# Rounding the convolved rows to their high part on ScalarE instead of VectorE, in the recurrent block of a two-layer diffusion backbone

## The chip, the cores and the metric

The kernel runs on one core of one Trainium2 chip. The metric is the device time of one launch in microseconds (us). A trace of one profiled execution gives start, length and idle time of each instruction on the engines: TensorE (PE, with its weight loads as PEld), VectorE (DVE), ScalarE (ACT), GpSimd (POOL) and SyncE (SP), which issues the DMAs. Each engine takes its instructions in the order in which the program wrote them; a wait at the head of an engine's queue holds everything behind it.

## What is computed

Two layers over 256 latent rows with a prefix of 256 context rows, width 1024. Layer 0 is neighbourhood attention and a dense SwiGLU. Layer 1, in which the change lies, is a bidirectional gated linear recurrence (1536 channels), followed by a top-2-of-8 expert SwiGLU. Cut to the recurrent block:

```python
g, xr = jnp.split(h @ w_in, 2, axis=-1)             # 1536 + 1536 columns
xc = dwconv(xr, conv_w, conv_b)                     # width 4, per channel
for d, rev in enumerate((False, True)):             # both directions
    r = sigmoid(blockdiag(xc, wa[d], ba[d]))        # 16 blocks of 96x96
    i = sigmoid(blockdiag(xc, wx[d], bx[d]))
    log_a = -8.0 * r * softplus(-lam[d])
    a, mult = exp(log_a), sqrt(-expm1(2.0 * log_a))
    hs += linear_scan(a, mult * (i * xc), h0, rev)  # h0: the context's last state
y = (gelu(g) * hs) @ w_out
```

## The kernel before

Matrix products with full precision are made of three passes. An operand is split into a high part (rounded to float32r) and a low part (the operand minus its high part), and `mm3` (lines 468 to 472) multiplies high by high, high by low and low by high. For weights, ScalarE makes the high part `whi` (line 370) from a landed tile `raw`, and VectorE the low part `wlo` (line 381); five such pairs are alive at a time.

The recurrent block holds its 1536 channels as 12 tiles of 128 channels by 512 columns (256 latent, 256 context). `MIX` (line 48) is the order in which the block is written down, and so the order on each engine: `g` is a tile of the gelu branch, `x` a tile of the convolved branch, `a` the gates of three tiles, `w` the output product.

`g0-4 x0-2 g5 a0 x3-5 g6-8 a1 x6-8 g9-10 x9 a2 x10-11 g11 a3 w...`

`x_tile(t)` multiplies (`pX`, PE), lets ScalarE do the convolution's centre tap with the bias (line 1387, `xcv`), VectorE the three other taps (line 1389, three instructions), and splits `xcv` into `xcs`: the high part (line 1395) and the low part (line 1396). `gates(q)` takes three x tiles through 12 block-diagonal products in PSUM (`pA`, 4 banks in turn); ScalarE empties each bank with a tanh (line 1423, `ri`), makes a second tanh from every other one (line 1426, `th`, 7 buffers), and VectorE multiplies (line 1429). A bank or a `th` buffer that is still in use holds up whoever wants it next.

`post(q)` puts the rest of the three tiles into a list, `todo`, from which `run(n)` writes pieces between later tiles: `rates` (Exp on ScalarE at line 1442, then lines 1443 and 1444 on VectorE), `roots` (Sqrt on ScalarE at line 1436, then line 1437 on VectorE), `scans` (lines 1448 to 1454, VectorE alone), `gated` (line 1461, `z`). So the leftovers of one group of tiles stand between the x tiles of the next. In particular the piece after x tile 3, 6 or 10 begins with Exp on ScalarE, preceded by a load of ScalarE's function table; and the scans of a group are written before x tile 9 while the gates of the group a2 are written after it.

Of the kernel before, what the change touches and what calls it, by code (L numbers as in the profile page):

```python
# [419 lines left out]
def body(tc, nc, es, a, out, upto, dbg):  # L420
# [940 lines left out]
    def win_mm(t, p, s):  # L1361
        u = st.need(("win", t))
        for k in range(KD):
            mm3(p, wt(u, k), hx(k, s), k == 0, k == KD - 1)
        st.done(("win", t))
# [14 lines left out]
    def x_tile(t):  # L1380
        p = psu("pX")
        win_mm(12 + t, p, slice(0, 512))
        xc_ = xv.tile([P, 512], F32, name="xcv", tag="xcv", bufs=4)
        o = xc_.rearrange("p (s t) -> p s t", s=2)
        r = p.rearrange("p (s t) -> p s t", s=2)
        cw = vv("cw", 4 * t, 4)
        nc.scalar.activation(o, r, AF.Identity, bias=vv("cb", t, 1), scale=cw[:, 2:3])
        for j, (d0, d1, s0, s1) in ((0, (2, NL, 0, NL - 2)), (1, (1, NL, 0, NL - 1)), (3, (0, NL - 1, 1, NL))):
            nc.vector.scalar_tensor_tensor(
                o[:, :, d0:d1], r[:, :, s0:s1], cw[:, j:j + 1], o[:, :, d0:d1], ALU.mult, ALU.add  # L1390
            )
        if t % 2 == 0:
            xs2[0] = rawm.tile([P, 2, 2, 512], F32R, name="xcs", tag="raw", bufs=RM // 2)
        xh, xl_ = xs2[0][:, t % 2, 0], xs2[0][:, t % 2, 1]
        nc.vector.tensor_copy(xh, xc_)
        nc.vector.tensor_tensor(xl_, xc_, xh.bitcast(F32), ALU.subtract)
        xc_t[t] = (xc_, xh, xl_)

# [111 lines left out]
    for i, (kind, n) in enumerate(MIX):  # L1510
# [3 lines left out]
        elif kind == "x":  # L1514
            if n == 0:
                st.lag = 0
                lp = pool(ls, "lp", 2)
                vs = ExitStack()
                xv = pool(vs, "xv", side="right")
            x_tile(n)  # L1520
            if n == 11:
                st.add_pool(hp, 4, wide=True)
# [551 lines left out]
```

## Time and profile before

| | us |
|---|---|
| median of 3 runs (lowest, highest) | 1827.32 (1821.88, 1831.45) |
| profiled execution | 1827.48 |
| its span, first to last instruction | 1825.5 |
| PE busy | 1733.7 (95%) |
| DVE busy | 1064.1 (58%) |
| ACT busy | 752.9 (41%) |
| POOL busy | 92.1 (5%) |

The shares are means over stages with different limits. The change lies between 726 and 913 us, in the recurrent block; from about 1050 us on the expert weights are streamed at 419 GB/s. A stage is read from its own stretch of the trace: which engine has no idle time in it, and what the others wait for. A row of the timeline gives start, length, engine, line, operation and tile, how many instructions are merged in it, and in brackets the idle time of the engine before it with what ended that.

### The profile page before, as it was taken

Reading aid. Unit: us, or ns where it says so; the run is one execution under the profiler, and the core shown is the slowest. Engines: PE = TensorE matmul, PEld = TensorE weight load, DVE = VectorE, ACT = ScalarE, POOL = GpSimd, SP = SyncE. Lnnn points to the kernel's source line nnn. Section 1 sums busy time; section 2 is a strip of 40 time slices with the busy share of each in tenths; the row PEclk is TensorE's granted clock in tenths of the full one; section 3 lists DMA queues with packets and bytes.
Section 4 is the critical chain, followed back from the end, with each engine's and each line's share of the span. In section 5 each row is a group of like instructions: output and inputs, shape, how many; then the busy total and the mean of one; then the engine's idle time right before and its main releaser. Section 6 shows DMA issues by size and latency. Waiting matters only on the chain.

```text
span 1825.5 us, 26013 instructions
## 1 busy us (share of the span) xinstructions
PE 1733.7 (95%) x9973; PEld 1289.3 (71%) x9973; DVE 1064.1 (58%) x1698; ACT 752.9 (41%) x1147; POOL 92.1 (5%) x126
## 2 busy tenths in 40 slices
PE   8999899999999999989898999999899999998997
PEld 6887568988788889877687766666566556655564
DVE  4784676886766437699878444453344344534342
ACT  4434654422222226666736433333334333433341
POOL 1001341200000003000010000000000000000000
PEclk9999999999999999999898999999999999999999
DMA  7444621364656223232475799999999999999996
GB/s 305 168 142 147 204 75 47 127 209 163 229 196 231 92 93 102 96 113 76 162 274 207 298 413 419 420 419 420 419 419 419 420 420 419 420 419 419 419 420 277
DMA packets 94963, 489.87 MB, mean 268 GB/s; under 512 B 10480, under 2 KB 15984, under 8 KB 55920
## 3 DMA queue, kind: packets, MB, share of 16 engines
q1 hardware_dynamic: 94688, 488.01, 68.9%
q8 instruction: 80, 1.31, 0.3%
q14 instruction: 51, 0.42, 0.1%
q10 hardware_dynamic: 144, 0.13, 0.0%
HBM read 487.05 MB, written 1.05 MB: 267 GB/s over the span
## 4 chain that ended last, share of the span: by engine, by line
PE 61%; DMA 24%; DVE 10%; ACT 3%; issue 1%; POOL 1%; SPq 0%; DVEq 0%; ACTq 0%; POOLq 0%
DMA raw<-moe_d 23%; PE ph L1808 10%; PE psa L470 4%; PE psa L471 4%; PE psa L472 4%; PE pY L1492 2%; PE pF L470 2%; PE pF L471 2%; PE pF L472 2%; PE ph L1896 2%; PE ph L1898 2%; PE ph L1897 2%; DVE wlo L381 2%; PE py L1828 1%; PE py L1829 1%
## 5 line engine op out<-in xcount | busy, mean ns | idle before, releaser
L381 DVE TENSOR_TENSOR wlo<-raw,whi 128x1024 fp32r<-128x1024 f32 x386 | 461.7, 1221 | 217.2 <-ACT whi L370 213.7
L370 ACT CAST whi<-raw 128x1024 fp32r<-128x1024 f32 x388 | 395.7, 1047 | 251.2 <-DMA raw<-moe_d 100.2
L1808 PE MATMUL ph<-raw,xs 128*64 128x256 f32 x2240 | 267.2, 390 | 33.7 <-ACT msil L1925 33.7
L1808 PEld LDWEIGHTS ph<-raw,xs 128*64 128x64 f32 x2240 | 155.7, 139 | 126.4 <-ACT msil L1925 47.8
L470 PE MATMUL psa<-hh,whi 128*128 128x512 f32 (+1 forms) x384 | 145.1, 378 | 0.0
L471 PE MATMUL psa<-hl,whi 128*128 128x512 f32 (+1 forms) x384 | 144.2, 376 | 0.7 <-DVE hl L721 0.6
L472 PE MATMUL psa<-hh,wlo 128*128 128x512 f32 (+1 forms) x384 | 143.8, 374 | 0.0
L1898 PE MATMUL ph<-wlo,xe 128*128 128x512 f32 x336 | 132.6, 395 | 4.4 <-DVE wlo L381 4.4
L1896 PE MATMUL ph<-whi,xe 128*128 128x512 f32 x336 | 134.2, 399 | 0.9 <-ACT whi L370 0.9
L1897 PE MATMUL ph<-whi,xe 128*128 128x512 f32 x336 | 131.9, 393 | 0.0
L1808 PE MATMUL ph<-raw,mgs 128*64 128x512 f32 (+1 forms) x608 | 128.1, 563 | 0.6 <-ACT mgs L1871 0.5
L1927 DVE TENSOR_TENSOR msil<-msil,ph 128x256 f32<-128x256 f32 x35 | 14.6, 418 | 157.3 <-PE ph L1808 144.0
L595 DVE SCALAR_TENSOR_TENSOR macc<-raw,c,macc 128x1024 f32<-128x1024 f32 x84 | 105.3, 1280 | 0.7
L1808 PEld LDWEIGHTS ph<-raw,mgs 128*64 128x64 f32 x608 | 40.6, 137 | 68.0 <-issue 63.2
L470 PEld LDWEIGHTS psa<-hh,whi 128*128 128x128 f32 x384 | 73.5, 191 | 14.4 <-issue 2.1
L471 PEld LDWEIGHTS psa<-hl,whi 128*128 128x128 f32 x384 | 73.5, 191 | 13.6 <-DVE hl L721 1.5
L472 PEld LDWEIGHTS psa<-hh,wlo 128*128 128x128 f32 x384 | 73.4, 191 | 12.6
L1898 PEld LDWEIGHTS ph<-wlo,xe 128*128 128x128 f32 x336 | 63.5, 189 | 20.0 <-DVE wlo L381 6.4
L470 PE MATMUL pF<-gh,whi 128*128 128x512 f32 (+1 forms) x208 | 74.8, 360 | 0.4 <-ACT gh L483 0.4
L471 PE MATMUL pF<-gl,whi 128*128 128x512 f32 (+1 forms) x208 | 74.3, 357 | 0.3 <-DVE gl L484 0.3
L483 ACT CAST mgh<-pgt 128x512 fp32r<-128x512 f32 x21 | 12.3, 586 | 150.5 <-PE pgt L1874 150.5
L472 PE MATMUL pF<-gh,wlo 128*128 128x512 f32 (+1 forms) x208 | 74.1, 356 | 0.0
(349 smaller groups left out, 3051.9 us busy)
## 6 DMA issues: line engine op xcount, KB each, us to landing
raw<-moe_d SPq DMA_DIRECT2D x304, 1024.0 KB, 17.4
raw<-f_d SPq DMA_DIRECT2D x66, 512.0 KB, 3.6
raw<-wm_d SPq DMA_DIRECT2D x64, 512.0 KB, 4.6
raw<-moe_d SPq DMA_DIRECT2D x60, 512.0 KB, 17.4
raw<-wmh_d SPq DMA_DIRECT2D x32, 512.0 KB, 8.1
raw<-qkv_d SPq DMA_DIRECT2D x24, 512.0 KB, 4.2
raw<-win_d SPq DMA_DIRECT2D x24, 512.0 KB, 3.5
raw<-gat_d SPq DMA_DIRECT2D x14, 512.0 KB, 3.7
```

The lines of the kernel that those rows point to most:

```text
L370: self.nc.scalar.copy(hi, self.raws[i][0])
L381: eng.tensor_tensor(lo, self.take(key), hi.bitcast(F32), ALU.subtract)
L470: nc.tensor.matmul(o, w[0], x[0], start=first, stop=False)
L471: nc.tensor.matmul(o, w[0], x[1], start=False, stop=False)
L472: nc.tensor.matmul(o, w[1], x[0], start=False, stop=last)
L595: nc.vector.scalar_tensor_tensor(m[2][s], w, c32[:, k, s:s + 1], m[2][s], ALU.mult, ALU.add)
L1492: nc.tensor.matmul(Y[m][:, 0:NL], u[:, (t % 8) * P:(t % 8) * P + P], z_t[k], start=(k == 0), stop=(k == NB - 1))
L1808: nc.tensor.matmul(o[h], x, w[h], start=first, stop=last, skip_group_check=True)
L1828: nc.tensor.matmul(ys[e][n], x[0], w[0], start=b, stop=False)
L1896: nc.tensor.matmul(acc[part], xh[:, k], w[0], start=(k == 0), stop=False)
L1897: nc.tensor.matmul(acc[part], xl_[:, k], w[0], start=False, stop=False)
L1898: nc.tensor.matmul(acc[part], xh[:, k], w[1], start=False, stop=(k == 7))
```

## The change

One line of `x_tile` is changed: the copy that rounds `xcv` to its high part is issued on ScalarE and no longer on VectorE.

```diff
         xh, xl_ = xs2[0][:, t % 2, 0], xs2[0][:, t % 2, 1]
-        nc.vector.tensor_copy(xh, xc_)
+        nc.scalar.copy(xh, xc_)
         nc.vector.tensor_tensor(xl_, xc_, xh.bitcast(F32), ALU.subtract)
```

It takes 12 instructions from VectorE's queue and puts 12 into ScalarE's, each at the place where it was written: behind line 1387 of its own tile, and ahead of whatever ScalarE does next. It reads `xcv` after VectorE's last tap, and VectorE's subtraction reads what it writes. The queues of PE, POOL and SP are the same.

ScalarE at x tile 3, the first tile after the gates a0 (`whi` is a weight's high part, `ri` the gate to be exponentiated):

```order
 L370 CAST whi<-raw 128x1024
 L1387 ACTIVATE xcv<-pX,vec 128x512
+L1395 CAST xcs<-xcv 128x512
 L1442 ACT_TABLE_LOAD
 L1442 ACTIVATE ri_6867<-ri_6867,sp_656 128x512
```

The table load and the Exps of `rates` now stand behind the cast; x tiles 6 and 10 read alike.

ScalarE at x tile 9, the tile ahead of the gates a2 (`pA` are the gate products in PSUM):

```order
 L370 CAST whi<-raw 128x1024
 L1387 ACTIVATE xcv<-pX,vec 128x512
+L1395 CAST xcs<-xcv 128x512
 L1423 ACTIVATE ri_7719<-pA,hb 128x512
 L1426 ACTIVATE th<-ri_7719,sp_655 128x512
```

Here the instruction that follows is the first that empties a bank of `pA` for the gates a2.

VectorE at the same x tile 9:

```order
 L1389 SCALAR_TENSOR_TENSOR xcv<-pX,vec,xcv 128x2x254
 L1389 SCALAR_TENSOR_TENSOR xcv<-pX,vec,xcv 128x2x255 x2
-L1395 CAST xcs<-xcv 128x512
 L1396 TENSOR_TENSOR xcs<-xcv,xcs 128x512
 L1429 SCALAR_TENSOR_TENSOR ri_7730<-ri_7730,xcv 128x512
```

The cast leaves, and nothing comes between the last tap and the subtraction; the same holds for all 12 tiles.

## Rows read from the trace of the kernel before

**Rows 1.** Chain that ended last, in order of time: start, length, what.

```profile
898.73 0.82 ACT th L1426
...
900.17 0.79 PE pA L470
```

**Rows 2.** Busy time by engine from x tile 3 to the last gates.

```profile
766.51:912.45 145.94, 127.95 (x596) 104.95 (x595) 135.63 (x202) 102.94 (x139) 0.00 (x0) 0.95 0.32 110
```

**Rows 3.** SP's DMA queue behind the last gates: a wait, and the issue.

```profile
SPq L305 <- PE pA L472: 3.7, 1, 3.7
...
910.95 1.84 SPq L305 DMA_DIRECT2D raw<-moe_d  x3
```

**Rows 4.** The line of the cast: count, then shortest, median, longest in ns.

```profile
L1395 DVE CAST xcs<-xcv x12: 426/428/429, 730.5 to 882.0; 128x512 fp32r<-128x512 f32 x12
```

**Rows 5.** Timeline, ACT and DVE, another split of 128x512 (layer 0's SwiGLU).

```profile
347.75 0.62 ACT L483 CAST gh<-fg 128x512 fp32r<-128x512 f32 x1 [0.83 <-DVE fg L1253]
...
348.41 0.69 DVE L484 TENSOR_TENSOR gl<-fg,gh 128x512 fp32r<-128x512 f32 x1 [0.69 <-ACT gh L483]
```

**Rows 6.** Timeline, DVE, x tile 2, then x tiles 3 to 5.

```profile
738.15 2.31 DVE L1389 SCALAR_TENSOR_TENSOR xcv<-pX,vec,xcv 128x508 f32<-128x508 f32 x3 [0.80 <-ACT xcv L1387]
...
767.33 2.31 DVE L1389 SCALAR_TENSOR_TENSOR xcv<-pX,vec,xcv 128x508 f32<-128x508 f32 x3 [3.30 <-ACT xcv L1387]
...
770.74 0.68 DVE L1443 SCALAR_TENSOR_TENSOR ri<-ri,th 128x512 f32<-128x512 f32 x1
...
776.13 2.31 DVE L1389 SCALAR_TENSOR_TENSOR xcv<-pX,vec,xcv 128x508 f32<-128x508 f32 x3
...
781.67 1.29 DVE L1437 TENSOR_TENSOR ri<-ri,th 128x512 f32<-128x512 f32 x2
...
784.01 2.31 DVE L1389 SCALAR_TENSOR_TENSOR xcv<-pX,vec,xcv 128x508 f32<-128x508 f32 x3
...
789.83 1.22 DVE L381 TENSOR_TENSOR wlo<-raw,whi 128x1024 fp32r<-128x1024 f32 x1
```

**Rows 7.** ACT's table load, Exp and Sqrt lines, and one weight cast.

```profile
767.31 1.28 ACT L1442 ACT_TABLE_LOAD   x1
...
781.87 1.03 ACT L370 CAST whi<-raw 128x1024 fp32r<-128x1024 f32 x1
...
L1442 ACT ACTIVATE ri<-ri,sp x24: 799/803/818, 768.6 to 915.1; 128x512 f32<-128x512 f32 x24
...
L1436 ACT ACTIVATE th<-th x24: 612/618/637, 775.9 to 919.9; 128x512 f32<-128x512 f32 x24
```

**Rows 8.** Timeline, ACT, gates a2 and x tile 10.

```profile
840.85 0.69 ACT L1423 ACTIVATE ri<-pA,hb 128x512 f32<-128x512 f32 x1 [0.28 <-PE pA L472]
...
851.94 0.81 ACT L1426 ACTIVATE th<-ri,sp 128x512 f32<-128x512 f32 x1 [7.00 <-DVE th L1454]
...
869.63 0.78 ACT L1387 ACTIVATE xcv<-pX,vec 128x512 f32<-128x512 f32 x1
```

**Rows 9.** Timeline, DVE, x tile 9 and x tile 10.

```profile
857.54 2.31 DVE L1389 SCALAR_TENSOR_TENSOR xcv<-pX,vec,xcv 128x508 f32<-128x508 f32 x3
...
870.86 2.31 DVE L1389 SCALAR_TENSOR_TENSOR xcv<-pX,vec,xcv 128x508 f32<-128x508 f32 x3
```

**Rows 10.** Timeline, PE, gates a2: products 5 to 7, and the eighth.

```profile
846.09 0.39 PE L470 MATMUL pA<-xcs,whi 128*128 128x512 f32 x1
...
849.95 0.39 PE L472 MATMUL pA<-xcs,wlo 128*128 128x512 f32 x1
854.32 0.79 PE L470 MATMUL pA<-xcs,whi 128*128 128x512 f32 x1 [3.99 <-ACT ri L1423]
```

**Rows 11.** Timeline, DVE and ACT, behind x tile 11.

```profile
885.20 1.29 DVE L1437 TENSOR_TENSOR ri<-ri,th 128x512 f32<-128x512 f32 x2
...
887.54 2.49 DVE L1437 TENSOR_TENSOR ri<-ri,th 128x512 f32<-128x512 f32 x4
...
882.41 0.39 ACT L1376 ACTIVATE ge<-pG 128x256 f32<-128x256 f32 x1
```

## The prediction, made blind

> **What bounds the kernel now.** I read the chain of waits first. From 767 us to 898.7 us nearly every link is a VectorE instruction; then it passes over ScalarE's tanh of line 1426, which had waited for a scan, to PE's gate products [rows 1]. The table of busy time says the same: from x tile 3 to the last gates VectorE works 135.63 of 145.94 us, ScalarE 102.94, PE 127.95 [rows 2]. So in this stretch the end is set by VectorE's queue, and PE, whose 95% over the whole span suggests otherwise, waits. Before x tile 3 VectorE still has air. After the last gates PE is the bound, and the first expert weights are issued only when PE has done with its last gate products [rows 3]. Every later load hangs on buffers that later work frees, so I count a delay of the last gates in full at the end.
>
> **What the change takes away.** 12 casts of 428 ns [rows 4]; with the hand-over to the next instruction each holds VectorE's queue for 0.46 us. That is 5.5 us, 4.1 us of it (9 tiles) on the chain.
>
> **What it adds per tile: a round trip.** The kernel has the same three steps elsewhere: in layer 0 VectorE multiplies, ScalarE casts 128x512 in 0.62 us, VectorE subtracts, and VectorE sits idle 0.69 us in between [rows 5]. Hand-overs cost 0.03 to 0.04 us each. In x_tile nothing stands between the last tap and the subtraction on VectorE, so VectorE waits 0.69 us where it worked some 0.49 us: 0.2 us worse per tile, before anything is queued up.
>
> **What it adds to ScalarE's queue.** Until now ScalarE did its centre tap and ran ahead; now it stands still until VectorE has finished that tile's three taps. What it does next comes late, and much of that is what VectorE or PE wants next. I follow that tile by tile.
>
> *x tiles 0 to 2.* The round trips, and weight casts that come behind them, cost VectorE a few tenths at each tile. The idle 0.80 us ahead of tile 2's taps [rows 6] takes up most, and the 3.30 us ahead of tile 3's taps show that VectorE is not yet the bound; I carry 0.4 us (bounds 0 to 0.8) into gates a0, whose products PE runs without a break up to x tile 3.
>
> *x tiles 3 to 5, on the chain.* Tile 3: the taps end at 767.33 + 2.31 = 769.64, and line 1443 followed at 770.74 [rows 6], because ScalarE had already loaded its table (767.31) and made Exp during the taps. Now cast (0.62), table load (1.28) and Exp (0.80) [rows 7] come one after the other behind the taps: 0.03 + 0.62 + 0.02 + 1.28 + 0.02 + 0.80 + 0.04 = 2.81 us instead of 1.10, **1.7 us late**. Tile 4: the taps end at 778.44 + 1.7 = 780.14, cast to 780.79, the fifth and sixth Exp to 782.35, table load to 783.64, first Sqrt (0.62) to 784.28; line 1437 starts at 784.32 instead of 781.67, **2.65 late**. ScalarE's second Sqrt ends at 784.81 and its weight cast (1.03, here 1.05) at 785.78; VectorE's `wlo` at 785.82 is 2.94 late. Tile 5: taps end at 786.32 + 2.94 = 789.26, cast to 789.91, four Sqrts to 792.12 (line 1437 follows each), weight cast to 793.1; VectorE's `wlo` at 793.14 instead of 789.83, **3.3 us late**. The scans behind it need nothing of ScalarE, and the `th` buffers and low weights that PE waits for come from this queue, so everything shifts by 3.3.
>
> *x tiles 6 to 8.* The same instructions in the same order: another 3.3 us. With the 0.4 from the start VectorE is 7.0 us late at tile 9.
>
> *x tile 9.* This is the largest term. ScalarE is done with the centre tap before 840.85, but VectorE comes to the other taps only at 857.54, behind the scans of the group before [rows 8, 9]. So far ScalarE uses that time: at 840.85 it begins to empty the banks of gates a2, and has emptied three when it stops at 851.94 for a `th` buffer (7.00 us of idle). PE gets through seven of the 12 products and stands 3.99 us until 854.32 [rows 10]. With the cast ahead of line 1423, ScalarE empties nothing until VectorE has reached and done the taps: 857.54 + 2.31 + 7.0 = 866.85, plus cast 0.65, plus the first emptying 0.69, with hand-overs 868.25. PE, with all four banks full, starts again there and not at 854.32: 13.9 late, and with eight products to do instead of five. Products 5 to 7 took 846.09 to 850.2 [rows 10], 4.1 us. The rest up to x tile 10's product is PE's own work then as now, so ScalarE's tap for tile 10 moves from 869.63 by 13.9 + 4.1 = **18.0 us**. VectorE, which had 0.4 us of backlog there, starts the taps of 870.86 17.6 late. The tile thus costs 10.6 beyond the 7.0.
>
> *x tiles 10 and 11.* Tile 10 repeats tile 3, 1.7. Tile 11 repeats the first half of tile 4, 0.95. Then the gelu tile g11 stands between the Sqrts: after the second Sqrt ScalarE has a weight cast (1.03), a table load (1.28), gelu (0.39), a table load (1.28) and the third Sqrt (0.62), 4.6 us [rows 7, 11]. Until now this ran beside VectorE; line 1437 came at 885.20 and again at 887.54, 2.34 apart [rows 11]. With ScalarE no longer ahead the gap is 4.6 us and some 0.5 for the second Sqrt, 5.1 us: 2.75 more. VectorE's last scans start 17.6 + 1.7 + 0.95 + 2.75 = 23.0 us late, and with them the `th` at 898.73 and PE at 900.17 [rows 1]. ScalarE comes to that tanh some 5 us before its buffer is free, so nothing else is later.
>
> **Sum.** 0.4 + 3.3 + 3.3 + 10.6 + 1.7 + 0.95 + 2.75 = 23.0 us. On the profiled execution's own 1827.48 (span 1825.5 and 2.0 around it), which is 0.2 us off the median of the runs shown, that gives 1850.5; I say 1850.
>
> **Unknown costs.** The clock: after the 4 us stop PE's first products took up to 0.79 us instead of 0.39 [rows 10], and the granted clock of the stage averages 0.95 [rows 2], so part of it ran at the lower level, 1.2 GHz. Whether a stop of some 16 us leaves PE there longer no row shows; between nothing and the length of products 5 to 7 (0 to 4 us), I take nothing beyond what the row after the shorter stop already holds, since by then ScalarE's emptyings also pace PE. At the far end the expert stage may give something back if loads run further ahead; bounds 0 to half the delay, I take 0 by [rows 3].
>
> **Rivals.** (1) *VectorE was the bound and is relieved.* 5.5 us less work, up to 4.1 of it on the chain: 1822 to 1823.5, which is not slower, and too little to be told from no change. The place is the pair last tap and subtraction; it decides if VectorE has at least 0.7 us of other work to do between them, or ScalarE's later work is never awaited. The order shows neither: the subtraction is the next instruction in all 12 tiles. The Trainium skill's Perfetto Trace Analysis, section Optimizing Scalar/DVE Operations, says that with DVE saturated, moving work to Scalar may make sense, and that DVE is faster where it has a performance mode. By that rule the time would be this rival's; the trace supports its premise (VectorE saturated) and also its caution (0.43 against 0.62 us), but the rule prices engine time and not the wait. (2) *Only the round trip counts*, ScalarE being idle enough to catch up: 12 x 0.2 = 2.4 us, 1830, no change that can be told. Against it: the Exp and the emptyings are awaited at once. (3) *Tile 9 costs only a round trip*, if gates a2 were held by the `th` buffers or VectorE anyway: 23.0 - 10.6 + 0.2 = 12.6, 1840. For it: ScalarE does stand 7.00 us there already. Against it: three banks were emptied before that stop. (4) *Half the delay is given back* in the expert stage: 1839. (5) *PE's lower clock and missed overlaps add* some 4 to 8 us: 1856. That the change does not do what it says is ruled out by the order of instructions.
>
> **How the numbers follow.** Forecast 0.62 (1845 to 1855), rival 3 0.13, rival 4 0.06, rival 5 0.08, rival 2 0.08, rival 1 0.03. The range 1837 to 1857 takes in the forecast, rivals 3 and 4 and about half of 5, and leaves out some 0.15. A measurement of this kernel tells about 0.5% (9 us) from no change, so rivals 1 and 2 are "same", 0.12 with some allowance for the measurement: faster 0.02, same 0.12, slower 0.86.
>
> **What would show it.** In the profile of the changed kernel: line 1395 on ScalarE 12 times at about 0.62 us, its waits for line 1389 long, the longest (over 15 us) at tile 9; line 1396 waiting 0.69 us for it; line 1443 waiting some 1.7 us for Exp at tiles 3, 6 and 10; PE standing 14 to 18 us for line 1423 in gates a2; the first expert load near 934 instead of 911. The forecast is wrong if PE's stop in gates a2 is under 8 us, if line 1443 finds Exp ready, or if the expert stage takes less time than before from its first load on.

## The result, and the profile after

The changed kernel takes 1849.87 us (median of 4 runs, 1848.37 to 1850.44), the kernel before in the same comparison 1827.86. The ratio is 1.0126, 95% interval 1.0109 to 1.0144: some 22 us slower, between 20 and 26. The profiled execution took 1848.37 with a span of 1846.4, 20.9 over the span before. In what follows, medians leave out the few launches that took 2466.94 us or more.

The cast of line 1395 as a group: duration, then what ended the idle time of its engine, then who waited for it.

```profile
L1395 ACT CAST xcs<-xcv x12: 617/620/622, 729.5 to 901.0; 128x512 fp32r<-128x512 f32 x12
its engine sat idle before it (us, times) until:
  DVE xcv L1389: 47.6, 12
who waited for it (us, times):
  DVE xcs L1396: 8.9, 12
...
  PE pA L470: 2.1, 1
```

The cast itself is 7.4 us of work in all. ScalarE stands 47.6 us in front of it, waiting for the taps. VectorE waits 0.74 us for each cast, against the 0.43 us that its own cast took [rows 4].

VectorE's timeline, x tiles 3 to 11 (start, length, instruction, count, idle time ahead and who ended it); its rows answer to [rows 6, 9, 11].

```profile
767.11 2.31 DVE L1389 SCALAR_TENSOR_TENSOR xcv<-pX,vec,xcv 128x508 f32<-128x508 f32 x3 [3.29 <-ACT xcv L1387]
770.17 0.69 DVE L1396 TENSOR_TENSOR xcs<-xcv,xcs 128x512 fp32r<-128x512 f32 x1 [0.74 <-ACT xcs L1395]
772.30 0.69 DVE L1443 SCALAR_TENSOR_TENSOR ri<-ri,th 128x512 f32<-128x512 f32 x1 [1.44 <-ACT ri L1442]
...
784.10 1.29 DVE L1437 TENSOR_TENSOR ri<-ri,th 128x512 f32<-128x512 f32 x2 [0.43 <-ACT th L1436]
...
863.83 2.30 DVE L1389 SCALAR_TENSOR_TENSOR xcv<-pX,vec,xcv 128x508 f32<-128x508 f32 x3
...
888.02 2.31 DVE L1389 SCALAR_TENSOR_TENSOR xcv<-pX,vec,xcv 128x508 f32<-128x508 f32 x3 [3.30 <-ACT xcv L1387]
...
910.10 2.50 DVE L1437 TENSOR_TENSOR ri<-ri,th 128x512 f32<-128x512 f32 x4 [2.41 <-ACT th L1436]
```

In the kernel before, none of the rows that answer to these but the first, 767.33, waited. Now VectorE waits for ScalarE at Exp, at Sqrt, at x tile 10's centre tap and behind the gelu tile. The taps of x tile 3 start within 0.22 us of where they did, those of x tile 10 17.2 us later.

The timeline of ScalarE around x tile 9 (centre tap, cast, first emptying) answers to [rows 8]:

```profile
850.87 0.79 ACT L1387 ACTIVATE xcv<-pX,vec 128x512 f32<-128x512 f32 x1
...
866.22 0.62 ACT L1395 CAST xcs<-xcv 128x512 fp32r<-128x512 f32 x1 [14.56 <-DVE xcv L1389]
866.75 0.68 ACT L1423 ACTIVATE ri<-pA,hb 128x512 f32<-128x512 f32 x1
```

And PE's, in gates a2, answers to [rows 10]:

```profile
848.88 0.80 PE L470 MATMUL pA<-xcs,whi 128*128 128x512 f32 x1 [3.77 <-ACT ge L1376]
...
867.48 0.80 PE L470 MATMUL pA<-xcs,whi 128*128 128x512 f32 x1 [11.79 <-ACT ri L1423]
```

Line 1423 is the first emptying of a gate's bank. It stands behind the cast, the cast behind the taps, and the taps behind the scans of the group before. Before, ScalarE had emptied three banks while VectorE was at those scans. Now it empties none, and PE stands twice: 3.77 us for a bank that a late gelu still holds, then 11.79 us until 867.48 instead of 854.32. SP's queue issues the first expert load 21.7 us later than in [rows 3]:

```profile
932.64 1.84 SPq L305 DMA_DIRECT2D raw<-moe_d  x3
```

### The profile page after: what moved, and what is told of

Same layout as the page of the kernel before. It is cut to its first block, busy times and chain, and to the rows that moved or that the text cites. A ratio compares the mean times of both kernels' runs of the same rounds, so it can differ in the third digit from the quotient of the medians.

```text
span 1846.4 us, 26007 instructions
## 1 busy us (share of the span) xinstructions
PE 1737.0 (94%) x9973; PEld 1290.7 (70%) x9973; DVE 1059.9 (57%) x1686; ACT 759.6 (41%) x1159; POOL 92.5 (5%) x126
## 4 chain that ended last, share of the span: by engine, by line
PE 59%; DMA 25%; DVE 9%; ACT 5%; issue 1%; POOL 1%; SPq 0%; DVEq 0%; ACTq 0%; POOLq 0%
DMA raw<-moe_d 24%; PE ph L1808 9%; PE psa L470 4%; PE psa L471 4%; PE psa L472 4%; PE pY L1492 2%; PE pF L470 2%; PE pF L471 2%; PE pF L472 2%; PE ph L1898 2%; PE ph L1896 2%; PE ph L1897 2%; DVE wlo L381 2%; PE psa L1168 1%; PE psa L1170 1%
## 5 line engine op out<-in xcount | busy, mean ns | idle before, releaser
L470 PE MATMUL pA<-xcs,whi 128*128 128x512 f32 x112 | 48.4, 432 | 29.9 <-ACT ri L1423 18.7
```

The costliest lines, as they stand in the source:

```text
L470: nc.tensor.matmul(o, w[0], x[0], start=first, stop=False)
```

## Which part of it costs what

Executions differ ahead of this stretch: among the profiled ones, programs that are alike up to there reach the taps of x tile 3 anywhere between 762.17 and 768.41 us. So the table counts from the start of these taps (T) in each trace, to the taps of x tiles 9 and 10, to the last four Sqrt products (the row `L1437 ... x4` above, other line numbers elsewhere) and to SP's first expert load (`moe_d`). The last column is from there to the end of the span. Each entry is the difference of two starts, the last column that of a start and the end of the span. What such a difference is worth can be read off too: with x tile 11 alone nothing is changed between T and the taps of x tile 10, and yet they come 0.12 us later than in the kernel before, and as late with x tiles 0 to 2, whose changes lie ahead of T.

| Kernel | T | to x9 | to x10 | to last Sqrt products | to first expert load | the rest |
|---|---|---|---|---|---|---|
| before | 767.33 | 90.21 | 103.53 | 120.21 | 143.62 | 914.55 |
| after (all 12) | 767.11 | 96.72 | 120.91 | 142.99 | 165.53 | 913.76 |
| x tiles 0 to 2 | 764.31 | 90.32 | 103.65 | 120.33 | 143.96 | 915.33 |
| x tiles 3, 6, 10 | 767.12 | 93.85 | 107.41 | 125.86 | 148.63 | 915.15 |
| x tiles 4, 5, 7, 8 | 766.06 | 93.24 | 106.56 | 123.23 | 145.86 | 914.08 |
| x tile 9 | 765.02 | 90.40 | 114.49 | 131.18 | 154.59 | 914.99 |
| x tile 11 | 762.17 | 90.32 | 103.65 | 123.95 | 145.09 | 913.84 |
| all but x tile 9 | 765.12 | 96.88 | 110.21 | 132.29 | 155.00 | 917.78 |
| added work, not held | 771.36 | 90.32 | 103.64 | 120.31 | 143.86 | 915.18 |
| added work, held | 764.89 | 98.76 | 122.83 | 144.73 | 167.36 | 914.05 |
| later place, ScalarE | 770.44 | 86.85 | 99.87 | 115.72 | 138.18 | 913.88 |
| later place, VectorE | 768.41 | 89.47 | 102.59 | 119.02 | 142.97 | 915.32 |

The theory: the loss is what stands behind the cast in ScalarE's queue, which is held until the taps are done. Rivals: ScalarE's own added work costs (12 x 0.62 us); each cast costs a fixed round trip; or gates a2 are held by the `th` buffers anyway.

### x tile 9 alone, and all but x tile 9

```diff
-        nc.scalar.copy(xh, xc_)
+        if t == 9:          # the other kernel: t != 9
+            nc.scalar.copy(xh, xc_)
+        else:
+            nc.vector.tensor_copy(xh, xc_)
```

Three lines more, so the gates' first emptying is line 1426 here, and VectorE's cast and subtraction are lines 1398 and 1399.

> Only x tile 9's cast stands on ScalarE; the eleven others stay on VectorE. Theory (ScalarE's in-order queue is held at the cast until VectorE has done that tile's taps, and what stands behind it comes late): ScalarE waits for line 1389 some 8 to 9 us at this one cast, from its centre tap of x tile 9 near 844 or later until the taps end at 857.54 + 2.31 = 859.85; PE's long stop for line 1423 in gates a2 ends near 861.3 instead of 854.3, with about three more products of 1.37 us behind it, so the taps of x tile 10 start 10 to 11 us later than 870.86 and the time is about 1838 (10.7 us over the kernel before). Rival A (the buffers `th` hold gates a2 anyway, so ScalarE's stop is free; only the round trip of 0.25 us is added): about 1828. Rival B (the tile is dear only when the tiles before it have already made VectorE late): 1 to 4 us, 1829 to 1832.

> Eleven casts on ScalarE, x tile 9's back on VectorE. Theory: everything of the change but the stop in gates a2: some 22 - 10.9 = 11 to 12 us over the kernel before, 1839 to 1840; PE's longest stop for line 1423 in gates a2 is back near 4 us, and the taps of x tile 10 start 6 to 7 us later than 870.86. Rival A (gates a2 are held by the `th` buffers anyway and tile 9's cast costs only its round trip): 1849 to 1850, no better than the changed kernel. Rival B (tile 9 is dear only behind late tiles): as the theory here.

Measured for x tile 9 alone: 1836.04 us against 1825.77, ratio 1.0044 (1.0027 to 1.0061). ScalarE's row at the cast, and PE's behind it:

```profile
857.82 0.62 ACT L1396 CAST xcs<-xcv 128x512 fp32r<-128x512 f32 x1 [19.39 <-DVE xcv L1389]
```

```profile
859.08 0.80 PE L470 MATMUL pA<-xcs,whi 128*128 128x512 f32 x1 [15.14 <-ACT ri L1426]
...
873.06 0.39 PE L470 MATMUL pX<-hh,whi 128*128 128x512 f32 x1
```

T is 2.31 us earlier in this trace, so PE restarts at 861.4 counted in times of the kernel before, as expected. From there to x tile 10's product it is 13.98 us, with 18 matmuls of line 470, where the kernel before has 12 of them and 9.67 us behind 854.32: work that had not been done ahead of the stop. To x tile 10 the stretch is 10.96 longer, to the expert load 10.97. One cast of twelve costs half of the change. The expectation of an 8 to 9 us hold was wrong: the hold began at the end of the centre tap and is 19.39. Rival B of the expectation, that the tile is dear only behind late tiles, falls here, since the tiles ahead of it were on time.

All but x tile 9: 1836.43 against 1825.77, ratio 1.0042 (1.0025 to 1.0059), which is less than the 11 to 12 us expected; these four runs lie between 1832.14 and 1839.98. In the trace the stretch is 11.38 longer, and x tile 9 to 10 takes 13.33 us, as before (13.32). With 10.97 + 11.38 = 22.35 against the changed kernel's 21.91, the two parts add up in the traces. The medians lie 10.27 and 10.66 us over the kernel before, 20.9 together against 22.0; the ratios of the timed runs, which are not those of the medians, sum to less, 1.0086. Rival A, that `th` buffers hold the gates anyway, falls with both.

### Three casts here or there

The condition is `t < 3`, `t in (3, 6, 10)`, `t in (4, 5, 7, 8)` or `t == 11` in the same four lines.

> Three casts on ScalarE, those of x tiles 0 to 2, where VectorE still has idle time ahead of the taps. Theory (the price is what waits behind the cast, not the cast's 0.62 us): VectorE waits 0.74 us at line 1396 three times, its idle ahead of tile 3's taps shrinks from 3.30 us, and the taps of x tile 3 start where they did (767.3): 0 to 0.4 us, about 1828. Rival (each cast on ScalarE costs the same, 22/12 = 1.8 us, or its own work 0.62 us): 1.9 to 5.5 us, 1829.7 to 1833.

> Three casts on ScalarE again, those of x tiles 3, 6 and 10, behind which ScalarE has a table load (1.28 us) and Exp (0.80 us) that VectorE wants next. Theory: line 1443 waits about 1.4 us for Exp in each of the three, and each tile costs 1.1 to 1.7 us more than before: 3.5 to 5.2 us in sum, about 1832. Rival (each cast on ScalarE costs its round trip of 0.25 us, or its own 0.62 us, wherever it is): 0.75 to 1.9 us, 1828.5 to 1829.7, the same as with x tiles 0 to 2.

> The four tiles not yet tried alone, x tiles 4, 5, 7 and 8, whose casts stand ahead of Exp, Sqrts and a weight cast. Theory: with the tiles before them on time the Exp and Sqrts are late by the round trip and one waited Sqrt at tiles 4 and 7 (0.95 us each) and by a round trip at tiles 5 and 8 (0.25 to 0.65 each): 2.4 to 3.2 us, so 146.0 to 146.8 us from the taps of x tile 3 to the first expert load, about 1829; the terms of all runs with some of the casts then add up to the changed kernel's. Rival (the terms don't add up, because a tile is dear only behind a late one): 0 to 1 us, under 144.6.

> Only x tile 11's cast on ScalarE, behind which Sqrts, a weight cast, two table loads and a gelu tile stand. Theory: 0.95 + 2.75 = 3.7 us by the prediction's terms, 2.9 to 3.7 us: from the taps of x tile 3 to the first expert load 146.5 to 147.3, about 1829 to 1830; line 1437 waits some 2.4 us for its third Sqrt. Rival (a cast costs its round trip of 0.25 us): 143.9.

Measured, as ratio to the kernel before: x tiles 0 to 2, ratio 1.0000 (0.9985 to 1.0015), 1827.18 us; x tiles 3, 6, 10, ratio 1.0028 (1.0014 to 1.0042), 1831.59; x tiles 4, 5, 7, 8, ratio 1.0019 (1.0009 to 1.0029), 1829.70; x tile 11, ratio 1.0013 (0.9996 to 1.0030), 1828.11. The times tell the second and third from no change, not the first and the last; the terms are read from the traces. In the first three tiles the cast is the same instruction, held as well and waited for as well:

```profile
L1396 ACT CAST xcs<-xcv x3: 618/622/623, 727.7 to 738.0; 128x512 fp32r<-128x512 f32 x3
its engine sat idle before it (us, times) until:
  DVE xcv L1389: 8.9, 3
who waited for it (us, times):
  DVE xcs L1399: 2.2, 3
```

It costs nothing that can be told (0.34 us to the expert load), since VectorE still has idle time ahead of x tile 3, 3.30 us in the kernel before [rows 6]. With x tiles 3, 6 and 10 VectorE's timeline shows what was expected:

```profile
772.31 0.69 DVE L1446 SCALAR_TENSOR_TENSOR ri<-ri,th 128x512 f32<-128x512 f32 x1 [1.44 <-ACT ri L1445]
...
825.22 0.69 DVE L1446 SCALAR_TENSOR_TENSOR ri<-ri,th 128x512 f32<-128x512 f32 x1 [1.44 <-ACT ri L1445]
```

That is 5.65 us to the Sqrt products, 1.8 to 1.9 a tile where 1.1 to 1.7 was expected, and 5.0 to the load. So the price of the same instruction runs from 0.1 us a tile to 11 us, by what is queued behind it and who wants that.

x tile 11 cost what was expected to the Sqrt products, 3.74 us, but 1.47 to the load, where 2.9 to 3.7 was expected: 2.27 us came back in the last gates. x tiles 4, 5, 7, 8 cost 3.02 and 2.24, the latter a little under the 2.4 to 3.2 expected. Up to the Sqrt products the parts sum to 0.12 + 5.65 + 3.02 + 10.97 + 3.74 = 23.5 against 22.78 for all twelve together. Most of the difference of 0.7 is the reference: all five parts are taken against one trace of the kernel before, in which this stretch is some 0.12 us shorter than where the same code runs in the traces of x tiles 0 to 2 and x tile 11. The sum holds that 0.12 five times and the whole holds it once.

What came back is PE's clock. Windows from the last gates' tanh that waits for its `th` buffer [rows 1] to the expert load (length, then PE, weight loads, VectorE, ScalarE and GpSimd busy with counts, PE's granted clock, DMA share, GB/s), of before, of after, with x tile 11 alone and with x tile 9 alone:

```profile
898.73:910.95 12.22, 10.78 (x37) 8.71 (x38) 8.52 (x14) 8.83 (x13) 0.00 (x0) 0.74 0.14 44
```

```profile
921.29:932.64 11.35, 9.91 (x37) 8.14 (x38) 8.51 (x14) 8.83 (x13) 0.00 (x0) 0.85 0.15 48
```

```profile
897.33:907.26 9.93, 8.49 (x37) 7.05 (x38) 8.51 (x14) 8.62 (x13) 0.00 (x0) 1.00 0.16 54
```

```profile
907.39:919.61 12.22, 10.78 (x37) 8.73 (x38) 8.52 (x14) 8.84 (x13) 0.00 (x0) 0.74 0.14 44
```

The same 37 matmuls take 10.78, 9.91, 8.49 and 10.78 us, and the window is shorter by just that; VectorE's work in it is the same, and ScalarE's nearly so (8.62 to 8.84). These differences are hardly chance from trace to trace, since they go with the order of the program. Where the cast of x tiles 10 and 11 stays on VectorE and no added cast holds ScalarE there, the granted clock of this window is 0.73 to 0.74 (the kernel before, x tiles 0 to 2, x tile 9, the added work that is not held, the later place on VectorE) and once 0.79 (x tiles 4, 5, 7, 8). In the other six traces of the table it is 0.85 to 1.00. What in the order decides it is not settled. The length of PE's stop just ahead doesn't tell it. In after PE's row is

```profile
922.73 0.80 PE L470 MATMUL pA<-xcs,whi 128*128 128x512 f32 x1 [4.58 <-ACT ri L1423]
```

and with x tile 9 alone, at the lower clock,

```profile
908.83 0.80 PE L470 MATMUL pA<-xcs,whi 128*128 128x512 f32 x1 [4.22 <-ACT ri L1426]
```

### ScalarE's work with the hold, and without

The kernel before, with twelve casts more on ScalarE. The first attempt read the product's bank, behind the taps in the code:

```diff
+        nc.scalar.copy(xh, p)
         nc.vector.tensor_copy(xh, xc_)
```

> The kernel before, with a cast of 128x512 more on ScalarE in each x tile, read from the product's bank right behind the centre tap, so that it waits for nothing of VectorE's taps; VectorE overwrites what it writes with its own cast, as before. It is ScalarE's added work without the hold. Theory (the hold costs, not the work): 0 to 1 us in the stretch from the taps of x tile 3 to the first expert load (143.6 to 144.6), about 1826 to 1827. Rival A (ScalarE's added work costs, 12 x 0.62 = 7.4 us): 1832 to 1834.

Measured: 1848.28 (three runs) against 1826.19, ratio 1.0133 (1.0109 to 1.0158), where 0 to 1 us was expected. ScalarE's row at x tile 9 tells why:

```profile
865.99 0.59 ACT L1395 CAST xcs<-pX 128x512 fp32r<-128x512 f32 x1 [14.95 <-DVE xcv L1389]
```

The added cast uses nothing that the taps make, but in the built program it waits for them, 49.4 us in all; both read one bank of PSUM, and that this is the reason no run shows by itself. So this run is the hold with nothing moved: VectorE keeps all its casts, and the time is that of the changed kernel, with 23.7 us more in the stretch. VectorE waits for ScalarE here as well, 7.8 us at the twelve casts with which it overwrites the added ones, so the hold comes together with a round trip as in the change. The run that had been meant reads a tile that is long ready, ahead of the taps in the code:

```diff
         nc.scalar.activation(o, r, AF.Identity, bias=vv("cb", t, 1), scale=cw[:, 2:3])
+        scr = xv.tile([P, 512], F32R, name="scr", tag="scr", bufs=1)
+        nc.scalar.copy(scr, hx(0, slice(0, 512))[0].bitcast(F32))
```

> The kernel before with a cast of 128x512 more on ScalarE in each x tile, behind the centre tap, from a tile that has long been ready into a scratch tile that nobody reads: ScalarE's added work, and it waits for nothing. (In the run with the cast from the product's bank the added cast did wait for the taps, since both read one bank; this is the run that was meant.) Theory (the hold costs, not the work): 0 to 1.5 us from the taps of x tile 3 to the first expert load (143.6 to 145.1), some of it where ScalarE's Exp or emptyings come 0.6 us later; about 1826 to 1828. Rival (ScalarE's added work costs, 12 x 0.6 = 7 us or more): 150 and over, 1832 to 1834.

Measured: 1828.12 against 1827.63, ratio 1.0003 (0.9988 to 1.0018), 0.24 us in the stretch. The added casts are nearly as long as those of the change, they wait for nothing, and nobody waits for them:

```profile
L1389 ACT CAST scr<-hh x12: 606/607/614, 731.2 to 881.0; 128x512 fp32r<-128x512 f32 x12
its engine sat idle before it (us, times) until:
who waited for it (us, times):
```

The two separate the causes: ScalarE's work alone costs nothing that can be told, and the wait for the taps, at the head of ScalarE's queue, costs as much as the change.

### Cast and subtraction later in both queues

`x_tile` no longer writes the cast and the subtraction down itself. It hands them back as `halves`, and these are written behind the pieces of later work that follow the tile (`run`), at x tile 9 only behind the gates a2. The edit is that against the changed kernel; its comment stands for the control's line, and `...` for lines left out.

```diff
-        nc.scalar.copy(xh, xc_)
-        nc.vector.tensor_tensor(xl_, xc_, xh.bitcast(F32), ALU.subtract)
         xc_t[t] = (xc_, xh, xl_)
+        def halves():
+            nc.scalar.copy(xh, xc_)     # the control: nc.vector.tensor_copy
+            nc.vector.tensor_tensor(xl_, xc_, xh.bitcast(F32), ALU.subtract)
+        return halves
...
-            x_tile(n)
+            halves = x_tile(n)
             ...
             run(4, 3)
+            if n == 9:
+                late = halves
+            else:
+                halves()
...
             post(n, gates(n))
+            if n == 2:
+                late()
```

> All twelve casts on ScalarE as in the changed kernel, but cast and subtraction stand behind the pieces of later work that follow a tile (behind Exp or the Sqrts at x tiles 3 to 8, 10 and 11; at x tile 9 behind all emptyings of gates a2), on both engines. Theory (the move loses only by what it holds up; ScalarE has the 0.62 us to spare): none of the waits of line 1389 <- ScalarE behind the casts, VectorE has work between its taps and the subtraction, and its queue is 0.43 to 0.46 us shorter per tile: from the taps of x tile 3 to the first expert load 143.62 us less 3 to 4, so 139.6 to 140.6, and about 1822 to 1824. Rival A (the 0.62 us of ScalarE's own work is what costs, wherever the cast stands): 1830 to 1835. Rival B (the stretch is set by PE or ScalarE as soon as VectorE has air): no change, 143.6 and 1826.

> The same later place of cast and subtraction, but the cast on VectorE as in the kernel before: what the place alone does. Both theory and rivals: within 0.5 us of the kernel before, 143.1 to 144.1 us from the taps of x tile 3 to the first expert load; if it gains 2 us or more, a gain of the later place with the cast on ScalarE is not the cast's.

Measured: with the cast on ScalarE 1821.77 us against 1826.19, ratio 0.9974 (0.9963 to 0.9986), faster than either kernel; the control on VectorE 1825.19, ratio 0.9995 (0.9982 to 1.0009). The cast's group in the faster one:

```profile
L1398 ACT CAST xcs<-xcv x12: 605/620/622, 732.8 to 880.9; 128x512 fp32r<-128x512 f32 x12
...
its engine sat idle before it (us, times) until:
  DVE xcv L1389: 14.7, 8
who waited for it (us, times):
  DVE xcs L1399: 2.2, 3
```

The same twelve casts of 620 ns: the hold is down from 47.6 to 14.7 us, and only the three of x tiles 0 to 2, left where they were because no later work is waiting there, make the subtraction wait. VectorE's timeline has the taps of x tiles 3 and 4, the latter's first instruction, 8.22 us apart:

```profile
770.44 2.31 DVE L1389 SCALAR_TENSOR_TENSOR xcv<-pX,vec,xcv 128x508 f32<-128x508 f32 x3 [3.30 <-ACT xcv L1387]
...
778.66 0.74 DVE L1389 SCALAR_TENSOR_TENSOR xcv<-pX,vec,xcv 128x508 f32<-128x508 f32 x1
```

In the control it is 8.68 (768.41 to 777.09), so 0.46 less; from x tile 4's to x tile 5's 7.28 against 7.75, 0.47 less. That is the gain per tile that the prediction worked out for the cast taken away. To the Sqrt products it comes to 3.30 us over the control, within the 3 to 4 expected. To the expert load it is 4.8 (138.18 against 142.97), but 1.5 of that is the last gates at a granted clock of 0.85 against 0.73, and not the cast. The stretch came out 1.4 us better than the 139.6 to 140.6 expected. Two terms had been put at nothing: the place alone, by which the control gained 1.19 us to the Sqrt products, and the last gates, which gave 0.95 against the kernel before.

## Why the prediction was right

It said 1850 and 23.0 us of delay at the last scans; measured are 1849.87, and 22.78 from T to the Sqrt products, for which the terms behind T make 22.6. The mechanism was right, each term behind T within 0.3 us. That the median lies within 0.2 us of the forecast is luck in part: T alone differs by some 6 us between executions, and the profiled execution lies 2 us under the sum. Term by term, from the table and the taps in between:

- **x tiles 0 to 2**, said 0.4: nothing. T is 0.22 us earlier than before, and counted from PE's product of x tile 0, which is 0.21 us earlier too, unchanged. The idle time ahead of x tile 3 took all of it. This term was too large, within its bounds.
- **x tiles 3 to 5 and 6 to 8**, said 3.3 each: the taps of x tile 6 come 3.35 later and those of x tile 9 6.51, so 3.16 for the second group. The round trip itself was under-sized, 0.74 us against 0.69.
- **x tile 9**, said 10.6: 17.38 at the taps of x tile 10, less 6.51, is 10.87; alone it is 10.96 to the same mark. Its largest step, the restart of PE at 868.25, was at 867.48, 13.4 late counted from T where 13.9 was said; the work left behind the restart cost 4.4 more and not 4.1 (14.09 us to x tile 10's product against 9.67). But the stop was read as one of 14 to 18 us for line 1423, and is two: 3.77 us for the gelu bank and 11.79 for line 1423. That ScalarE's late queue also keeps PE's banks shared with gelu tiles was not in the working. It cost nothing here, since the products that it delayed would have stood in the longer stop behind it.
- **x tile 10**, said 1.7: 1.77 (19.15 at x tile 11's taps, less 17.38). **x tile 11**, said 0.95 + 2.75: 3.63. Line 1443 waits 1.44 us, not the "some 1.7" that was named as a sign: 1.7 is how late it comes, and VectorE's own longer round trip is part of that.
- **Behind the last scans**, said to give nothing back: the last gates gave 0.87 by PE's clock and the expert stage 0.79 (914.55 to 913.76). The prediction had named an expert stage that takes less time than before as a sign of being wrong, and taken literally it is there; but all these traces lie between 913.76 and 917.78, the added work that is held, delayed as much, takes 914.05, and 0.79 is too little to be told from that spread. With the 0.22 at the start, 22.78 - 0.87 - 0.79 - 0.22 = 20.9, the difference of the spans. So the profiled execution lies 2 us under the sum, and the first expert load came at 932.64 instead of "near 934".

The rivals. (1), VectorE relieved at 1822 to 1823.5: not with this order, but it named the point from which it decides, other work between last tap and subtraction, and the kernel that provides it takes 1821.77. The Trainium skill's Perfetto Trace Analysis, section Optimizing Scalar/DVE Operations, says that with DVE saturated, offloading work to Scalar may make sense. The traces agree for that kernel (0.46 us per tile) and disagree for the change: the same 0.62 us of ScalarE's work gives some 3.4 us against its control (1821.77 against 1825.19) or takes 22, by where it stands in the queue. (2) and (3) fall with x tile 9 alone, which costs 10.97 us. (4), half given back, was 1.7 us of 22. (5), PE's lower clock: the first 4 us behind the 11.79 us stop of after, and behind the 3.99 us stop of before [rows 10], are

```profile
867.48:871.48 4.00, 4.00 (x10) 3.21 (x11) 1.02 (x3) 3.97 (x6) 0.00 (x0) 0.54 0.00 0
```

```profile
854.32:858.32 4.00, 4.00 (x11) 3.22 (x12) 3.90 (x6) 3.93 (x6) 0.00 (x0) 0.63 0.01 2
```

A granted clock of 0.54 against 0.63 over 4 us is 0.4 us of PE's time. In the next 4 us it is 1.00 in both, so the longer stop costs no more, and in the last gates the clock gave time back.

What stays open: what in the order of the program sets the granted clock of the last gates; some 0.2 us between the sum of the parts and the whole that the reference doesn't explain; and why the timed ratios of the two halves (1.0044 and 1.0042) sum to less than the whole's when their traces do not.

## What to carry to other kernels

Before an instruction is moved to an engine that looks idle, list what stands behind its new place and what it waits for: here the price was the time by which those came late where someone wanted them, and not its own length. Moved together with its consumer, to a place where its input was ready and the old engine had other work in between, the same instruction paid. Count from a mark just ahead of the changed stretch in each trace, so that small terms show that whole times cannot.

## What had not been expected of the hardware

In these traces a VectorE instruction that needs the result of the one just ahead starts later than one that doesn't. The timeline of the kernel before, and that of the control with the later place:

```profile
769.67 0.43 DVE L1395 CAST xcs<-xcv 128x512 fp32r<-128x512 f32 x1
770.13 0.69 DVE L1396 TENSOR_TENSOR xcs<-xcv,xcs 128x512 fp32r<-128x512 f32 x1
770.74 0.68 DVE L1443 SCALAR_TENSOR_TENSOR ri<-ri,th 128x512 f32<-128x512 f32 x1
```

```profile
768.41 2.31 DVE L1389 SCALAR_TENSOR_TENSOR xcv<-pX,vec,xcv 128x508 f32<-128x508 f32 x3 [3.30 <-ACT xcv L1387]
770.64 0.68 DVE L1447 SCALAR_TENSOR_TENSOR ri<-ri,th 128x512 f32<-128x512 f32 x1
```

The dependent cast starts 0.03 us after the taps end (767.33 + 2.31 = 769.64); the independent line 1447 starts 0.08 us before that end (770.72), and so does line 1443 behind the subtraction. The later place replaces one dependent hand-over by an independent one, 0.11 us in each of 9 tiles, which is most of the control's 1.19 us.

The second thing is that a delay can come with a higher clock further on: the same last gates ran at granted clocks between 0.73 and 1.00, and gave 0.9 of after's 22.8 us back.
